# One-hots of a gate table stored contiguously per token, with PSUM written in steps of four

## The chip, the cores and the metric

One Trainium2 chip, one core of it. The metric is the device time of one launch in microseconds, lower is better. Engines are named as the profile names them: PE (TensorE; PEld its weight loads), DVE (VectorE), ACT (ScalarE), POOL (GpSimd), SP (SyncE, which only issues DMAs here).

## What is computed

A decoder trunk of two layers over 512 tokens of width 1024: a mixer of four kinds of attention, then a PEER expert layer with 16384 experts. The change lies in the expert layer alone:

```
v1, i1 = top_k(s1, 16);  v2, i2 = top_k(s2, 16)          # per token and head, 128 keys each
top_s, top_j = top_k(v1[..., :, None] + v2[..., None, :], 16)
eid  = take_along_axis(i1 * 128 + i2, top_j)             # 8 heads x 16 = 128 experts per token
gate = softmax(top_s)
act  = gelu(einsum('cd,ced->ce', h, u[eid]))
out  = einsum('ce,ced->cd', gate * act, v[eid])
```

The kernel does this in a dense way for the first 384 tokens (three blocks of 128): it multiplies all tokens with all experts and weights the result with a *gate table*. For a token t the table is a 128 x 128 matrix: entry (a, b) is the gate of expert a * 128 + b, or zero. It is the product of two one-hot matrices, one of them scaled by the gates.

## The kernel before

The expert layer, per layer of the trunk, has a *stage* in which the gate table is built while the first experts' products with u already run, and a long stage after it that multiplies by the table and by v.

Each token block is turned by PE so that the 128 picks of a token lie on the partitions (`turn`). `turned_out` (L1614) stores the two numbers of each pick as `iT` (float16) and its gate as a float16 pair `gT` (high and low part, with `gF` and `gL` in float32). Then, for each batch b of eight tokens, 48 batches per layer:

- `g_ones` (L1628, DVE) compares the numbers with a row of 0 to 127 (`iota4`) and writes both one-hots of eight tokens, tile `o`: 2048 elements per partition.
- `g_scale` (L1635) multiplies the one-hot of the first number by the high (q = 0) and by the low (q = 1) part of the gate, tile `og`. It is one DVE instruction of 1024 elements, or, on ACT, eight of 128 with the token's gate as the scale.
- `g_mm` (L1648, PE, twice per batch): for each of four tokens two matmuls of 128 x 128 (high and low part added up), into a quarter of one PSUM bank `psa`.
- `g_out` (L1656, ACT) evicts that bank of four tokens into `gs`, in which the 32 tokens of a group are innermost. Every eighth eviction completes a group, and `g_put` (SP) sends it to `gdram`.

Meanwhile PE computes `u_mm` of one expert after another (24 matmuls of 384 columns, `psb`), for which ACT writes `uh` (L1347) and DVE `ul` (L1350), and ACT applies the gelu (`act`, L1363). Only 27 experts run beside the table; four more are held back until the last table matmul. DVE also decodes the picks of the later token blocks (`oh`, `pr`, `cid`, `ts`).

The order of all this on each engine is fixed when the program is built: the class `Plan` simulates it with costs written in the source, and `plan.run()` emits the instructions in the order found. The costs of the table's steps are these:

```
one = plan.add(due, lambda b=b: g_ones(b), ("W", 1.135), after=(ids_,), take=("o",))
hi = plan.add(due + 1, lambda e, b=b: g_scale(b, 0, E[e]), [("W", 0.602), ("S", 2.4)], after=(one, gts), take=("og",))
lo = plan.add(due + 1, lambda e, b=b: g_scale(b, 1, E[e]), [("W", 0.602), ("G", 2.3), ("S", 2.4)][:LA], after=(hi,))
```

Tile `o` has three buffers and `og` two, so work on batch b + 2 can enter `og` only when the matmuls of batch b are done.

After the stage, `gq_load` (L1799) reads the table back from `gdram`, `w_mul` (L1804) multiplies it with `act`, and the products with v follow.

Of the kernel before, what the change touches and what calls it, by code (L numbers as in the profile page):

```python
# [12 lines left out]
F16 = mybir.dt.float16  # L13
# [3 lines left out]
AF = mybir.ActivationFunctionType  # L17
ALU = mybir.AluOpType
# [22 lines left out]
GL = (3, 2, 3, 2, 2)  # L41
OA = (1, 0)
GSC = 2.0 ** 14
# [52 lines left out]
def bc(ap, shape):  # L96
    return ap.to_broadcast(shape)
# [1229 lines left out]
def peer(nc, tc, I, l, xd, fh, fl, h3, closing, q0, w012, both, wq_mm, right, hp, up, small, bank, mm3, iota128, pos, ident, dram, grow, ada, more, rows_out):  # L1327
    V, S, G, PE, SY = nc.vector, nc.scalar, nc.gpsimd, nc.tensor, nc.sync
# [35 lines left out]
    with tc.tile_pool(name=f"Q{l}", bufs=1) as qp:  # L1364
# [4 lines left out]
        wp = wcm.__enter__()  # L1369
# [105 lines left out]
        for h in range(8):  # L1475
            t0 = 10.2 * (h - 1)
            if h > 2:
                loads[h] = plan.add(t0 - 16, lambda h=h: wq_load(h), ("Q", 3.2), take=("wr",))
                wsplit[h] = []
                for half in range(2):  # L1480
                    a = plan.add(t0 - 7 + half, lambda h=h, half=half: wq_part(h, half, S), ("S", 1.0), after=(loads[h], wtake[h] if half else None), take=("w",) if half == 0 else ())
# [19 lines left out]
            for i in range(NT):  # L1501
# [6 lines left out]
                b = plan.add(at + 0.5, lambda h=h, i=i: key_best(h, i), ("V", 2.03), after=(m, lasts[-1] if lasts else None),  # L1508
                             take=("top",) if i == 0 else (), give=(("b" if h < KB else "a", src),) if h < KB or i % 2 else ())
# [7 lines left out]

        def turn_over():

            nonlocal wp, dp, iT, gT, gL, gF, iota4, pos8  # L1520
            wcm.__exit__(None, None, None)
            for cm in closing:
                cm.__exit__(None, None, None)
            rcm, rp = right(tc.tile_pool(name=f"ring{l}", bufs=1))
            ring.append(rp)
            cms.extend([rcm, tc.tile_pool(name=f"Q2{l}", bufs=1), tc.tile_pool(name=f"G{l}", bufs=1), tc.manual_schedule()])
            wp, dp = cms[1].__enter__(), cms[2].__enter__()
            cms[3].__enter__()
            iT = wp.tile([128, 96, 2, 4], F16, name="iT")
            gT = wp.tile([128, 2, 384], F16, name="gT")  # L1530
            gL, gF = (wp.tile([128, 384], F32, name=q) for q in ("gL", "gF"))
            iota4 = wp.tile([128, 128, 4], F16, name="iota4")
            G.tensor_copy(iota4, bc(iota128[:, :, None], [128, 128, 4]))
            pos8 = wp.tile([128, sum(NSEL), 8], F16, name="pos8")
            G.tensor_copy(pos8, bc(pos[:, :, None], [128, sum(NSEL), 8]))

        dp = iT = gT = gL = gF = iota4 = pos8 = None
        ready = plan.add(B0, turn_over, ("none", 0), after=list(kmm.values()) + dense)
        if True:
            picked, cids, ohs, prs, turned = {}, {}, {}, {}, {}  # L1540
# [73 lines left out]
            def turned_out(i, part):  # L1614
                cs, ps = slice(i * 128, (i + 1) * 128), turned[i]
                if part == 0:
                    V.tensor_copy(iT[:, 32 * i:32 * i + 32].rearrange("p g a t -> p a g t"), ps[:, 0:256].rearrange("p (a g t) -> p a g t", a=2, t=4))
                elif part == 1:
                    S.activation(gF[:, cs], ps[:, 256:384], AF.Copy, scale=GSC)
                    S.activation(gT[:, 0, cs], gF[:, cs], AF.Copy)  # L1620
                else:
                    V.tensor_sub(gL[:, cs], gF[:, cs], gT[:, 0, cs])
                    V.tensor_copy(gT[:, 1, cs], gL[:, cs])

            gst, gps, oo, gg = {}, {}, {}, {}
            NG = NTG * TG // 4

            def g_ones(b):  # L1628

                o = oo[b] = dp.tile([128, 4, 128, 4], F16, name="o", tag="o", bufs=GL[0])  # L1630
                shp = [128, 4, 128, 4]
                V.tensor_tensor(out=o, in0=bc(iota4[:, None], shp), op=ALU.is_equal,
                                in1=bc(iT[:, 2 * b:2 * b + 2].rearrange("p g a t -> p (g a) t")[:, :, None, :], shp))

            def g_scale(b, q, eng):  # L1635

                if q == 0:
                    gg[b] = dp.tile([128, 2, 2, 128, 4], F16, name="og", tag="og", bufs=GL[1])
                h, o = gg[b], oo[b].rearrange("p (g a) c t -> p g a c t", a=2)[:, :, 0]
                g = gT[:, q, 8 * b:8 * b + 8].rearrange("p (g t) -> p g t", t=4)  # L1640
                if eng is S:
                    for t in range(8):
                        g, t4 = divmod(t, 4)
                        S.activation(h[:, q, g, :, t4], oo[b][:, 2 * g, :, t4], AF.Copy, scale=(gL if q else gF)[:, 8 * b + t:8 * b + t + 1])  # L1644
                else:
                    eng.tensor_mul(h[:, q], o, bc(g[:, :, None, :], [128, 2, 128, 4]))

            def g_mm(j):  # L1648
                b, g = divmod(j, 2)
                o, h = oo[b], gg[b]  # L1650
                gps[j] = bank("a")
                for t in range(4):
                    for q in range(2):
                        PE.matmul(gps[j][:, t * 128:(t + 1) * 128], lhsT=o[:, 2 * g + 1, :, t], rhs=h[:, q, g, :, t], start=q == 0, stop=q == 1)  # L1654

            def g_out(j):  # L1656
                tg, t4 = divmod(j, TG // 4)
                if t4 == 0:
                    gst[tg] = dp.tile([128, 128, TG], F32, name="gs", tag="gs", bufs=GL[4])
                S.activation(gst[tg][:, :, 4 * t4:4 * t4 + 4].rearrange("p a t -> p t a"), gps.pop(j).rearrange("p (t a) -> p t a", t=4), AF.Copy, scale=1 / GSC)  # L1660

            def g_put(tg):
                SY.dma_start(gdram[tg], gst.pop(tg))
# [2 lines left out]
            turns, a, f = [], None, None  # L1666
            for i in range(NT):
                due, d = B0 + QD[i], QD[4]
# [3 lines left out]
                for q in range(4):  # L1672
                    a = plan.add(due + d * q, lambda e, i=i, q=q: ids(i, q, E[e]), [("G", 0.2 * len(SELB[q]) + NSEL[q] / 60), ("W", 0.08 * len(SELB[q]) + NSEL[q] / 240)],
                                 after=(head, a), take=("cid",))
                    b = plan.add(due + d * (1 + q), lambda i=i, q=q: places(i, q), dv(16 * NSEL[q], True), after=(t,), take=("oh",))
                    c = plan.add(due + d * (2 + q), lambda i=i, q=q: chosen(i, q), dv(16 * NSEL[q], True), after=(a, b), take=("pr",), give=(("cid", a), ("oh", b)))
                    red.append(plan.add(due + d * (3 + q), lambda i=i, q=q: decoded(i, q), ("W", 0.2 + 22 * NSEL[q] / 960), after=(c,), give=(("pr", c),)))
                f = plan.add(due + d * 7, lambda i=i: finish(i), ("V", 1.5), after=red + [ex, f], give=(("p", head),) if i == 3 else ())
                if i < 3:
                    f = plan.add(due + d * 8, lambda i=i: turn(i), ("PE", 0.65), after=(f,), take=("a",), give=(("p", head),))  # L1680
                    n = plan.add(due + d * 8, lambda i=i: turned_out(i, 0), dv(256), after=(f,))
                    b = plan.add(due + d * 8, lambda i=i: turned_out(i, 1), ("S", 0.5), after=(f,))
                    c = plan.add(due + d * 8, lambda i=i: turned_out(i, 2), ("V", 0.45), after=(b, n), give=(("a", f),))
# [106 lines left out]
    with tc.tile_pool(name=f"D{l}", bufs=1) as dp, ExitStack() as order:  # L1790
# [136 lines left out]
        with tc.tile_pool(name=f"X{l}", bufs=1) as xp:  # L1927
# [28 lines left out]
            if state is None:  # L1956
                scale, rest = evac(3)
                for i in range(2):
# [4 lines left out]
                    scale, rest = nxt  # L1963
# [152 lines left out]
```

## Time and profile before

| | |
|---|---|
| median of 3 runs | 3342.16 us (3340.18 to 3348.39) |
| the profiled execution | 3341.59 us, span of the core 3339.8 us |
| busy share of the span | PE 95%, PEld 84%, DVE 77%, ACT 45%, POOL 26% |
| mean granted TensorE clock | 0.971 of full speed |
| instructions | 48260 |

The span runs from the first to the last instruction. The table's stage is some 200 us of it per layer: about 520 to 720 us in the first layer and about 2170 to 2368 us in the second. A share over the whole span says little about it, so stretches of it are read by themselves below. Where the timeline gives one row for several instructions (x4), its length goes from the first start to the last end; instructions of one engine overlap a little, so the pace of a run is the distance from start to start, and not the length of one.

### The profile page before, as it was taken

The numbers are of one execution on the slowest core, as the hardware profiler recorded it, in microseconds if no ns is written. First come the engines' busy times: TensorE is split into PE (matmuls) and PEld (weight loads), VectorE is DVE, ScalarE is ACT, GpSimd is POOL, SyncE is SP. The second block draws the span as 40 slices with busy tenths as digits, with TensorE's granted clock in tenths as the row PEclk, the third lists the DMA queues.
The fourth block names the chain that finished last, engine by engine and source line by source line (L and its number), as shares of the span: only waits on it lengthen the run. The fifth ranks groups of instructions, "written<-read, shape, count | busy, mean of one in ns | idle before, by whom it ended". The sixth has DMA issues, their size and how long they took to land.

```text
span 3339.8 us, 48260 instructions
## 1 busy us (share of the span) xinstructions
PE 3183.5 (95%) x17540; PEld 2816.0 (84%) x17540; DVE 2585.4 (77%) x5528; ACT 1516.9 (45%) x2763; POOL 851.9 (26%) x682
## 2 busy tenths in 40 slices
PE   6999999979999999999999999998899999999998
PEld 6876879869989999998888668897799899999987
DVE  7767798858878888786666868988578787878856
ACT  3267527873333333333432864289533333333333
POOL 1300210004433343341022002100234344444400
PEclk9999999869999999999999999997899999999999
DMA  8402304459889989896654032144688899999954
GB/s 281 145 9 95 128 33 152 177 217 334 324 323 336 347 322 335 323 352 232 201 177 142 1 133 103 51 163 184 255 316 328 311 336 321 326 325 325 323 183 163
DMA packets 291343, 762.77 MB, mean 228 GB/s; under 512 B 23832, under 2 KB 130968, under 8 KB 285984
## 3 DMA queue, kind: packets, MB, share of 16 engines
q1 hardware_dynamic: 217376, 491.22, 42.3%
q0 software_dynamic: 73728, 268.47, 21.8%
q8 instruction: 137, 2.24, 0.3%
q14 instruction: 102, 0.84, 0.1%
HBM read 700.86 MB, written 58.74 MB: 227 GB/s over the span
## 4 chain that ended last, share of the span: by engine, by line
PE 75%; DVE 11%; ACT 8%; DMA 4%; issue 2%; POOL 0%; SPq 0%; DVEq 0%; ACTq 0%; POOLq 0%
PE psa L204 12%; PE psa L205 12%; PE psa L203 12%; PE psb L203 10%; PE psb L205 9%; PE psb L204 9%; ACT gs L1660 3%; PE psa L1654 2%; ACT og L1644 2%; PE psa L863 2%; PE psa L896 1%; DMA gq<-gdram 1%; DVE s L1437 1%; DMA wr<-in_w_in 1%; ACT P L877 1%
## 5 line engine op out<-in xcount | busy, mean ns | idle before, releaser
L203 PE MATMUL psb<-bh,uh 128*128 128x384 f32 x2048 | 692.0, 338 | 3.0 <-ACT act L1363 1.2
L205 PE MATMUL psb<-bh,ul 128*128 128x384 f32 x2048 | 688.9, 336 | 3.0 <-DVE ul L1350 3.0
L204 PE MATMUL psb<-bl,uh 128*128 128x384 f32 x2048 | 687.4, 336 | 0.0
L203 PE MATMUL psa<-vh,wdh 128*128 128x512 f32 x1512 | 590.8, 391 | 16.5 <-ACT wdh L1815 16.5
L205 PE MATMUL psa<-vh,wdl 128*128 128x512 f32 x1512 | 594.1, 393 | 0.0
L204 PE MATMUL psa<-vl,wdh 128*128 128x512 f32 x1512 | 593.8, 393 | 0.0
L1750 POOL DMA_INDIRECT gt<-in_peer_u,eid x256 | 341.6, 1334 | 726.3 <-DVE gt L1770 233.7
L1815 ACT ACTIVATE wdh<-act 128x384 fp32r<-128x384 f32 x252 | 132.1, 524 | 862.2 <-PE psa L204 640.6
L1750 POOL DMA_INDIRECT gt<-in_peer_v,eid x256 | 322.7, 1261 | 425.3 <-DVE a L1775 195.7
L203 PEld LDWEIGHTS psb<-bh,uh 128*128 128x128 f32 x2048 | 386.6, 189 | 13.2 <-DVE arow L250 2.6
L204 PEld LDWEIGHTS psb<-bl,uh 128*128 128x128 f32 x2048 | 386.1, 189 | 7.3
L205 PEld LDWEIGHTS psb<-bh,ul 128*128 128x128 f32 x2048 | 385.5, 188 | 4.7 <-DVE ul L1350 4.3
L1350 DVE TENSOR_TENSOR ul<-ur,uh 128x1024 fp32r<-128x1024 f32 x246 | 301.6, 1226 | 100.1 <-ACT uh L1347 87.8
L1816 DVE TENSOR_TENSOR wdl<-act,wdh 128x384 fp32r<-128x384 f32 x252 | 140.9, 559 | 286.6 <-ACT wdh L1815 272.1
L203 PEld LDWEIGHTS psa<-vh,wdh 128*128 128x128 f32 x1512 | 285.3, 189 | 72.2 <-ACT wdh L1815 17.1
L205 PEld LDWEIGHTS psa<-vh,wdl 128*128 128x128 f32 x1512 | 285.0, 188 | 60.1
L1827 DVE TENSOR_TENSOR vl<-vr,vh 128x1024 fp32r<-128x1024 f32 x252 | 307.8, 1221 | 33.0 <-ACT vh L1824 22.7
L204 PEld LDWEIGHTS psa<-vl,wdh 128*128 128x128 f32 x1512 | 285.1, 189 | 56.1
L1775 DVE SCALAR_TENSOR_TENSOR a<-gt,w,a 128x1024 f32<-128x1024 f32 x254 | 325.6, 1282 | 0.8
L1770 DVE SCALAR_TENSOR_TENSOR gt<-gt,h 128x1024 f32<-128x1024 f32 x256 | 310.9, 1220 | 0.0
L1347 ACT ACTIVATE uh<-ur 128x1024 fp32r<-128x1024 f32 x256 | 268.4, 1049 | 76.0 <-PE psb L204 64.2
L1363 ACT ACTIVATE act<-psb 128x384 f32<-128x384 f32 x256 | 126.8, 495 | 340.3 <-PE psb L205 340.2
(387 smaller groups left out, 5374.2 us busy)
## 6 DMA issues: line engine op xcount, KB each, us to landing
ur<-in_peer_uT SPq DMA_DIRECT2D x256, 512.0 KB
vr<-in_peer_v SPq DMA_DIRECT2D x256, 512.0 KB
gdram<-gs SPq DMA_DIRECT2D x24, 2048.0 KB
gq<-gdram SPq DMA_DIRECT2D x64, 768.0 KB
O<-in_ada_w SPq DMA_DIRECT2D x48, 512.0 KB
gt<-in_ada_w SPq DMA_DIRECT2D x32, 512.0 KB
wr<-in_w_q SPq DMA_DIRECT2D x14, 1024.0 KB
wr<-in_w_out SPq DMA_DIRECT2D x16, 512.0 KB
```

What stands on the lines that cost most here:

```text
L203: PE.matmul(ps, lhsT=wh, rhs=mh, start=first, stop=False)
L204: PE.matmul(ps, lhsT=wh, rhs=ml, start=False, stop=False)
L205: PE.matmul(ps, lhsT=wl, rhs=mh, start=False, stop=last)
L1347: S.activation(uspl[e][0], uraw[e], AF.Copy)
L1350: eng.tensor_sub(uspl[e][1], uraw.pop(e), uspl[e][0])
L1363: S.activation(acts[e], ups.pop(e)[:, :384], AF.Gelu_apprx_tanh)
L1750: G.indirect_dma_start(out=t, out_offset=None, in_=I["peer_u" if kind == "u" else "peer_v"], in_offset=bass.IndirectOffsetOnAxis(ap=eid3[: ...
L1770: V.scalar_tensor_tensor(t, t, 1.0, h3, op0=ALU.mult, op1=ALU.mult, accum_out=d3[:, s:s + 1])
L1775: V.scalar_tensor_tensor(a3, t, w3[:, s:s + 1], a3, op0=ALU.mult, op1=ALU.add)
L1815: S.activation(wh, w, AF.Copy)
L1816: V.tensor_sub(wl, w, wh)
L1827: V.tensor_sub(vspl[e][1], vraw.pop(e), vspl[e][0])
```

## The change

The one-hots of a token become contiguous (token, then which of the two numbers, then 128 columns), where before four tokens were interleaved element by element. For that the numbers and gates are stored twice side by side (`iT` and `gT` end in a dimension of 2), the row of 0 to 127 once (`iota16`, seen as 64 pairs), and DVE's operands are described in innermost runs of 2 elements, where they were runs of 4. PE then reads both its operands with step 1 (before: step 4) and writes each token's 128 columns into PSUM with a step of four columns (before: contiguous). ACT's eviction reads the bank in order and writes runs of four neighbouring words into `gs` (before: single words, 128 bytes apart).

```
-            iT = wp.tile([128, 96, 2, 4], F16, name="iT")
-            gT = wp.tile([128, 2, 384], F16, name="gT")
+            iT = wp.tile([128, 384, 2, 2], F16, name="iT")
+            gT = wp.tile([128, 2, 384, 2], F16, name="gT")
...
-            G.tensor_copy(iota4, bc(iota128[:, :, None], [128, 128, 4]))
+            G.tensor_copy(iota16, iota128.rearrange("p (c d) -> p c d", d=2))
...
-                    V.tensor_copy(iT[:, 32 * i:32 * i + 32].rearrange("p g a t -> p a g t"), ps[:, 0:256].rearrange("p (a g t) -> p a g t", a=2, t=4))
+                    V.tensor_copy(iT[:, cs].rearrange("p t a d -> p a t d"), bc(ps[:, 0:256].rearrange("p (a t) -> p a t", a=2)[:, :, :, None], [128, 2, 128, 2]))
...
-                    S.activation(gT[:, 0, cs], gF[:, cs], AF.Copy)
+                    S.activation(gT[:, 0, cs], bc(gF[:, cs, None], [128, 128, 2]), AF.Copy)
...
-                o = oo[b] = dp.tile([128, 4, 128, 4], F16, name="o", tag="o", bufs=GL[0])
-                shp = [128, 4, 128, 4]
-                V.tensor_tensor(out=o, in0=bc(iota4[:, None], shp), op=ALU.is_equal,
-                                in1=bc(iT[:, 2 * b:2 * b + 2].rearrange("p g a t -> p (g a) t")[:, :, None, :], shp))
+                o = oo[b] = dp.tile([128, 8, 2, 128], F16, name="o", tag="o", bufs=GL[0])
+                shp = [128, 16, 64, 2]
+                V.tensor_tensor(out=o.rearrange("p t a (c d) -> p (t a) c d", d=2), in0=bc(iota16[:, None], shp), op=ALU.is_equal,
+                                in1=bc(iT[:, 8 * b:8 * b + 8].rearrange("p t a d -> p (t a) d")[:, :, None, :], shp))
...
-                        S.activation(h[:, q, g, :, t4], oo[b][:, 2 * g, :, t4], AF.Copy, scale=(gL if q else gF)[:, 8 * b + t:8 * b + t + 1])
+                        S.activation(h[:, q, t], o[:, t], AF.Copy, scale=(gL if q else gF)[:, 8 * b + t:8 * b + t + 1])
                 else:
-                    eng.tensor_mul(h[:, q], o, bc(g[:, :, None, :], [128, 2, 128, 4]))
+                    pair = lambda x: x.rearrange("p t (c d) -> p t c d", d=2)
+                    eng.tensor_mul(pair(h[:, q]), pair(o), bc(gT[:, q, 8 * b:8 * b + 8, None], [128, 8, 64, 2]))
...
-                        PE.matmul(gps[j][:, t * 128:(t + 1) * 128], lhsT=o[:, 2 * g + 1, :, t], rhs=h[:, q, g, :, t], start=q == 0, stop=q == 1)
+                        PE.matmul(gps[j].rearrange("p (a t) -> p a t", t=4)[:, :, t], lhsT=o[:, 4 * g + t, 1], rhs=h[:, q, 4 * g + t], start=q == 0, stop=q == 1)
...
-                S.activation(gst[tg][:, :, 4 * t4:4 * t4 + 4].rearrange("p a t -> p t a"), gps.pop(j).rearrange("p (t a) -> p t a", t=4), AF.Copy, scale=1 / GSC)
+                S.activation(gst[tg][:, :, 4 * t4:4 * t4 + 4], gps.pop(j).rearrange("p (a t) -> p a t", t=4), AF.Copy, scale=1 / GSC)
```

The planner's costs are not touched, and no instruction moves: each engine issues the same number of instructions in the same order, with other access patterns. A piece of ACT's order in the first layer shows it, where the third token block is turned (`gF` and `gT` are its gates).

```order
 L1363 ACTIVATE act<-psb 128x384
-L1644 ACTIVATE og<-o,gL 128x128 x8
-L1660 ACTIVATE gs<-psa 128x4x128 x3
+L1642 ACTIVATE og<-o,gL 128x128 x8
+L1659 ACTIVATE gs<-psa 128x128x4 x3
 L1619 ACTIVATE gF<-psa 128x128
```

Eight scalings and three evictions stand in the same places; the eviction's pattern turns from four tokens of 128 columns to 128 columns of four tokens, and the source lines shift by one or two.

## Rows read from the trace of the kernel before

**Rows 1.** The page: busy time, share and instructions of each engine.

```profile
PE 3183.5 (95%) x17540; PEld 2816.0 (84%) x17540; DVE 2585.4 (77%) x5528; ACT 1516.9 (45%) x2763; POOL 851.9 (26%) x682
```

**Rows 2.** Windows, all engines: start and end, length, busy time (instructions), clock.

```profile
541.00:641.00 100.00, 98.92 (x656) 95.78 (x654) 81.34 (x141) 86.12 (x149) 5.74 (x2) 0.97 0.49 180
641.00:722.00 81.00, 61.95 (x436) 52.60 (x434) 61.84 (x96) 79.98 (x152) 0.00 (x0) 0.62 0.42 175
...
2290.00:2368.00 78.00, 58.96 (x420) 49.62 (x419) 60.84 (x94) 77.97 (x150) 0.00 (x0) 0.63 0.41 169
```

**Rows 3.** The same windows for the evictions into `gs` alone: ACT's busy time.

```profile
641.00:722.00 81.00, 49.97 (x51) 0.62 0.42 175
```

**Rows 4.** Timeline of ACT: start, length, instruction, count.

```profile
658.49 2.66 ACT L1644 ACTIVATE og<-o,gL 128x128 f16<-128x128 f16 x8
660.89 3.90 ACT L1660 ACTIVATE gs<-psa 128x512 f32<-128x512 f32 x4
664.60 2.66 ACT L1644 ACTIVATE og<-o,gL 128x128 f16<-128x128 f16 x8
```

**Rows 5.** Timeline of PE beside experts.

```profile
613.71 0.34 PE L205 MATMUL psb<-bh,ul 128*128 128x384 f32 x1
613.88 2.06 PE L1654 MATMUL psa<-og,o 128*128 128x128 f16 x16
```

**Rows 6.** Timeline of PE without experts, with its idle time ahead and what ended it.

```profile
659.07 4.42 PE L1654 MATMUL psa<-og,o 128*128 128x128 f16 x32 [1.90 <-ACT og L1644]
```

**Rows 7.** Timeline of DVE in the same loop.

```profile
661.51 0.69 DVE L1646 TENSOR_TENSOR og<-o,gT 128x1024 f16<-128x1024 f16 x1 [1.43 <-PE psa L1654]
662.12 2.51 DVE L1632 TENSOR_TENSOR o<-iota,iT 128x2048 f16<-128x2048 f16 x2
664.54 0.68 DVE L1646 TENSOR_TENSOR og<-o,gT 128x1024 f16<-128x1024 f16 x1
...
665.67 0.69 DVE L1646 TENSOR_TENSOR og<-o,gT 128x1024 f16<-128x1024 f16 x1
```

**Rows 8.** Chain that ended last, behind the table's last matmul: start, length.

```profile
720.00 6.99 DMA gdram<-gs
...
728.40 16.84 DMA gq<-gdram
...
745.27 0.57 DVE act L1806
```

**Rows 9.** Timelines of ACT in the mixer: contiguous writes.

```profile
200.02 1.05 ACT L802 ACTIVATE PT<-psa 128x512 f32<-128x512 f32 x2
200.97 0.38 ACT L877 ACTIVATE P<-P,nm 128x128 f32<-128x128 f32 x1
...
235.90 1.27 ACT L886 ACTIVATE P<-P,rz 128x128 f32<-128x128 f32 x4
```

**Rows 10.** Instructions on tile `o` (ns: shortest/median/longest), and `ul` by form.

```profile
L1654 PE MATMUL psa<-og,o x1536: 273/297/303, 525.6 to 2362.9; 128*128 128x128 f16 x192
L1644 ACT ACTIVATE og<-o,gL x352: 531/565/635, 532.1 to 2360.4; 128x128 f16<-128x128 f16 x176
L1646 DVE TENSOR_TENSOR og<-o,gT x146: 678/687/697, 525.0 to 2359.5; 128x1024 f16<-128x1024 f16 x146
L1632 DVE TENSOR_TENSOR o<-iota,iT x96: 1211/1219/3444, 521.1 to 2353.8; 128x2048 f16<-128x2048 f16 x96
...
L1350 DVE TENSOR_TENSOR ul<-ur,uh 128x1024 fp32r<-128x1024 f32 x246 | 301.6, 1226 | 100.1 <-ACT uh L1347 87.8 <-issue 12.2
```

**Rows 11.** PE's matmuls by form: count, busy us, mean ns of one.

```profile
L203 PE MATMUL psb<-bh,uh 128*128 128x384 f32 x2048 | 692.0, 338 | 3.0 <-ACT act L1363 1.2 <-ACT uh L1347 1.1 <-DVE arow L250 0.8
L203 PE MATMUL psa<-vh,wdh 128*128 128x512 f32 x1512 | 590.8, 391 | 16.5 <-ACT wdh L1815 16.5
```

**Rows 12.** Chain that ended last, early in the stage.

```profile
551.20 3.71 ACT gs L1660 x4
...
555.29 0.69 PE psb L203
```

More of the change, by code (lines that the diff above doesn't have):

```diff
@@ L1518, in turn_over @@
         def turn_over():
-            nonlocal wp, dp, iT, gT, gL, gF, iota4, pos8
+            nonlocal wp, dp, iT, gT, gL, gF, iota16, pos8
             wcm.__exit__(None, None, None)
@@ L1528, in turn_over @@
             cms[3].__enter__()
-            iT = wp.tile([128, 96, 2, 4], F16, name="iT")
-            gT = wp.tile([128, 2, 384], F16, name="gT")
+            iT = wp.tile([128, 384, 2, 2], F16, name="iT")
+            gT = wp.tile([128, 2, 384, 2], F16, name="gT")
             gL, gF = (wp.tile([128, 384], F32, name=q) for q in ("gL", "gF"))
-            iota4 = wp.tile([128, 128, 4], F16, name="iota4")
-            G.tensor_copy(iota4, bc(iota128[:, :, None], [128, 128, 4]))
+            iota16 = wp.tile([128, 64, 2], F16, name="iota16")
+            G.tensor_copy(iota16, iota128.rearrange("p (c d) -> p c d", d=2))
             pos8 = wp.tile([128, sum(NSEL), 8], F16, name="pos8")
             G.tensor_copy(pos8, bc(pos[:, :, None], [128, sum(NSEL), 8]))
-        dp = iT = gT = gL = gF = iota4 = pos8 = None
+        dp = iT = gT = gL = gF = iota16 = pos8 = None
         ready = plan.add(B0, turn_over, ("none", 0), after=list(kmm.values()) + dense)
@@ L1616, in turned_out @@
                 if part == 0:
-                    V.tensor_copy(iT[:, 32 * i:32 * i + 32].rearrange("p g a t -> p a g t"), ps[:, 0:256].rearrange("p (a g t) -> p a g t", a=2, t=4))
+                    V.tensor_copy(iT[:, cs].rearrange("p t a d -> p a t d"), bc(ps[:, 0:256].rearrange("p (a t) -> p a t", a=2)[:, :, :, None], [128, 2, 128, 2]))
                 elif part == 1:
                     S.activation(gF[:, cs], ps[:, 256:384], AF.Copy, scale=GSC)
-                    S.activation(gT[:, 0, cs], gF[:, cs], AF.Copy)
+                    S.activation(gT[:, 0, cs], bc(gF[:, cs, None], [128, 128, 2]), AF.Copy)
                 else:
-                    V.tensor_sub(gL[:, cs], gF[:, cs], gT[:, 0, cs])
-                    V.tensor_copy(gT[:, 1, cs], gL[:, cs])
+                    V.tensor_sub(gL[:, cs], gF[:, cs], gT[:, 0, cs, 0])
+                    V.tensor_copy(gT[:, 1, cs], bc(gL[:, cs, None], [128, 128, 2]))
             gst, gps, oo, gg = {}, {}, {}, {}
@@ L1628, in g_ones @@
             def g_ones(b):
-                o = oo[b] = dp.tile([128, 4, 128, 4], F16, name="o", tag="o", bufs=GL[0])
-                shp = [128, 4, 128, 4]
-                V.tensor_tensor(out=o, in0=bc(iota4[:, None], shp), op=ALU.is_equal,
-                                in1=bc(iT[:, 2 * b:2 * b + 2].rearrange("p g a t -> p (g a) t")[:, :, None, :], shp))
+                o = oo[b] = dp.tile([128, 8, 2, 128], F16, name="o", tag="o", bufs=GL[0])
+                shp = [128, 16, 64, 2]
+                V.tensor_tensor(out=o.rearrange("p t a (c d) -> p (t a) c d", d=2), in0=bc(iota16[:, None], shp), op=ALU.is_equal,
+                                in1=bc(iT[:, 8 * b:8 * b + 8].rearrange("p t a d -> p (t a) d")[:, :, None, :], shp))
             def g_scale(b, q, eng):
                 if q == 0:
-                    gg[b] = dp.tile([128, 2, 2, 128, 4], F16, name="og", tag="og", bufs=GL[1])
-                h, o = gg[b], oo[b].rearrange("p (g a) c t -> p g a c t", a=2)[:, :, 0]
-                g = gT[:, q, 8 * b:8 * b + 8].rearrange("p (g t) -> p g t", t=4)
+                    gg[b] = dp.tile([128, 2, 8, 128], F16, name="og", tag="og", bufs=GL[1])
+                h, o = gg[b], oo[b][:, :, 0]
                 if eng is S:
                     for t in range(8):
-                        g, t4 = divmod(t, 4)
-                        S.activation(h[:, q, g, :, t4], oo[b][:, 2 * g, :, t4], AF.Copy, scale=(gL if q else gF)[:, 8 * b + t:8 * b + t + 1])
-                else:
-                    eng.tensor_mul(h[:, q], o, bc(g[:, :, None, :], [128, 2, 128, 4]))
+                        S.activation(h[:, q, t], o[:, t], AF.Copy, scale=(gL if q else gF)[:, 8 * b + t:8 * b + t + 1])
+                else:
+                    pair = lambda x: x.rearrange("p t (c d) -> p t c d", d=2)
+                    eng.tensor_mul(pair(h[:, q]), pair(o), bc(gT[:, q, 8 * b:8 * b + 8, None], [128, 8, 64, 2]))
             def g_mm(j):
```

## The prediction, made before the changed kernel ran

> **What bounds the kernel now.** I read the page first: PE is busy for 95% of the span [rows 1], which would say that only PE's work counts. But the change lies in one stage of some 200 us per layer, so I cut that stage into stretches. Up to 641 us PE is busy for 98.92 of 100 us, beside ACT's 86.12 and DVE's 81.34: PE interleaves experts with table matmuls, and PE ends last. [...] So each layer has a stretch A bound by PE and a stretch B bound by ACT.
>
> In stretch B, ACT's timeline repeats every 6.11 us (658.49 to 664.60): eight scalings at a pace of 2.40/8 = 0.30 us, then four evictions at 3.71/4 = 0.93 us [rows 4]. One loop serves two batches. PE waits 1.90 us in it for ACT's scalings [rows 6], DVE waits 1.43 us for PE [rows 7]. Behind the stage the chain of waits goes from ACT's last eviction through the DMA of the last group (720.00, 6.99 us) and the load of the table (16.84 us) to DVE's first multiplication at 745.27 [rows 8]. Nothing there waits for the held experts, so what ACT's last eviction gains, the rest of the layer gains too.
>
> **The change part by part**, for one layer.
>
> *The eviction.* It keeps its 512 elements and its place, but writes runs of four words. Nearest row with contiguous writes from PSUM: two evictions of 128x512 start at 200.02 and ACT's next instruction at 200.97, so a pace of 0.48 [rows 9]. Bounds are 0.48 and today's 0.93; I take 0.48, since a run of four neighbours is nearer to a contiguous row than to single words 128 bytes apart.
>
> *The scalings on ACT.* Today one takes 565 ns [rows 10] but the next starts 0.30 us later. In the mixer four contiguous ones of 128x128 with the same kind of scale take 1.27 us together, and one such instruction 0.38 [rows 9]: a pace of (1.27 - 0.38)/3 = 0.30. So contiguity does not lift the pace; it can shorten the delay of the first result, by up to 565 - 380 = 0.18 us. Bounds 0.28 and 0.30: no gain in ACT's work.
>
> *What the loop becomes.* ACT's own work falls from 6.11 to 2.40 + 4 x 0.48 = 4.32 us. DVE's is about 4.85 us (661.51 to 665.67, plus 0.69, with a short wait for a buffer in it) [rows 7]. But the order is fixed, and a chain through ACT and PE closes the loop: first scaling to first matmul 0.58 us (658.49 to 659.07, [rows 4, 6]), seven more scalings 2.10, then the other batch's 16 matmuls at PE's pace of 0.117, which is 1.87, the length of the last one 0.30 [rows 10], and its eviction 0.48: together 5.33 us, or 5.15 with the shorter first result. I take 5.25. That saves 0.86 per loop. The stretch has 51 evictions [rows 3]: ten such loops, then a tail that ends in seven evictions in a row. Loops: -8.6 us. In the tail the evictions shrink by 7 x 0.45 = 3.2, and the one between the last two sets of scalings by another 0.45: -3.6. Together -12.2. Counter-check: 51 evictions x 0.45 are 23 us of ACT's work, of which the chain hands back 10 x (5.25 - 4.32) = 9.3, which leaves -13.7. I take -12.5.
>
> *Early in the stage* four evictions (3.71 us) hold ACT, and PE's next expert starts at 555.29 right behind them [rows 12]. Four at 0.48 would release PE up to 1.8 us earlier; I count -1.7.
>
> *The matmuls.* Their number stays: 768 per layer, half of 1536 [rows 10], of which 51 x 8 = 408 belong to stretch B and 360 to stretch A. Sixteen take (2.06 - 0.30)/15 = 0.117 us each [rows 5]. What the new patterns do, no row shows, so I bound it. From below: an expert's matmul of 384 columns starts 0.17 us before its successor (613.71 to 613.88), 0.45 ns per column, so 128 columns could pass in 0.058 us. That today's pace is not near this has a sign in the lengths: 384 columns take 338 ns and 512 take 391 [rows 11], 0.41 ns per column; carried down to 128 that is 232 ns, and the table's matmuls take 297 [rows 10]. Something costs them 65 ns, and the stepped operands may be it. From above: ACT's stepped writes cost 0.93/0.48 = 1.9 times the contiguous ones; as a factor on today's matmul that is 0.226 us. PE loses two stepped inputs and gets one stepped output. I take a pace of 0.113, near today's row, because one stepped operand remains: 360 x 0.004 = -1.4 us in stretch A; in stretch B it is within the 5.25.
>
> [...] No run here shows a matmul with a stepped output so far.
>
> *DVE.* `g_ones` takes 1219 ns for 2048 elements and a scaling 687 ns for 1024, while `ul`, with 4-byte elements, takes 1226 ns for 1024 [rows 10]: the 16-bit operations run at twice the elements per time, in runs of 4. With runs of 2 I take the same lengths; the other bound is the pace of `ul`, 1.2 ns per element, 2.3 and 1.23 us. [...]
>
> *Storing in pairs* writes 256 more elements in the copy of the numbers and 128 more in those of the gates, three times per layer. By `ul`'s row 256 elements are 0.3 us; only the first block's copy lies ahead of the first one-hot. +0.3. POOL's smaller copy of the 0-to-127 row gives nothing: POOL is busy for 5.74 of 100 us in stretch A and on none of the chains above [rows 2].
>
> Sum per layer: -12.5 - 1.7 - 1.4 + 0.3 = -15.3 us; two layers -30.6. The profiled execution took 3341.59 us (span 3339.8), 0.6 below the median of 3342.16, so the forecast is 3311 us. A measurement of this kernel can tell about 0.3%, 10 us, from no change.
>
> **The rivals.**
>
> *PE gets quick.* If the 65 ns are due to the stepped inputs and a stepped output costs nothing, the pace goes towards 0.058. Stretch A could lose 360 x 0.059 = 21 us, but DVE is busy for 81.34 of 100 there with a fixed order, so I grant 13. In stretch B the chain falls below DVE's work and the loop ends near 4.85: ten loops -12.6, tail -4.6. With the early -1.7 and the +0.3 that is -31.6 per layer, 3278 us, and 3262 if all 21 come through. For it: the lengths of rows 11. Against it: one stepped operand remains.
>
> *PE gets slow* (the other side). Each written column costs more than today's, up to 0.226 us per matmul. PE ends last in stretch A, so every nanosecond counts there: 360 x 0.109 = +39 us. In stretch B PE's two matmuls per token (0.45) then outlast a scaling (0.30), and the loop grows to about 0.6 + 8 x 0.45 + 16 x 0.226 + 0.8 = 8.6 us, +25 over ten loops. Per layer some +65, 3470 us at that bound. It decides from where the costs eat the -13.9 of the other terms: about 360 + 10 x 18 + 20 = 560 matmuls lie on the path, so at 0.117 + 0.025 = 0.142 us. [...]
>
> *DVE loses its double pace on runs of two.* 48 one-hots at +1.07 and 73 scalings at +0.54 are 91 us of DVE work per layer in two stretches where DVE is idle for 18.7 + 19.2 = 38 us [rows 2]; if all of that were filled, +53 per layer, 3448 us. Against it: the pace is the same to a few ns for `og` and `o` in runs of 4, and nothing in the rows hints at a limit on the run.
>
> *The eviction doesn't get shorter*, since its runs of four still lie 128 bytes apart: the loop stays at 6.11 and only small terms are left, 3340 us.
>
> **How the numbers follow.** The forecast (matmul pace 0.100 to 0.130, eviction near 0.5) gets 0.50; its own range is 3298 to 3323. PE quick 0.26, PE slow 0.13, DVE at single pace 0.05, eviction unchanged 0.06. Predicted is the likeliest, 3311. Faster by over 0.3%: 0.50 + 0.26 + 0.02 of PE slow (paces between 0.130 and 0.135) = 0.78. Within 0.3%: the unchanged eviction and the paces around the break-even, 0.07. Slower: 0.15. The range takes in all of the forecast and nearly all of PE quick, down to 3262, and reaches up to 3345 for the unchanged eviction; outside are most of PE slow, DVE's loss and a rest, 0.19.
>
> **What the new profile would show.** Eviction right: a pace near 0.48 where it was 0.93. Loop right: ACT's sets of scalings some 5.2 us apart, and ACT waiting for PE before its last evictions. Matmuls: 16 in about 1.8 us beside an expert; 0.9 to 1.3 would be PE quick, over 2.3 PE slow. DVE right: `o` near 1.22 and `og` near 0.69 us. Wrong would be the whole reading if the stage shrinks and the first multiplication after the table's load does not come earlier by as much.

## The result, and the profile after

| | before | changed |
|---|---|---|
| median of 4 runs each | 3341.47 us | 3296.93 us (3293.22 to 3299.51) |
| ratio | | 0.9862, 95% interval 0.9845 to 0.9879 |
| profiled execution | 3341.59 us, span 3339.8 | 3297.31 us, span 3295.5 |
| mean granted TensorE clock | 0.971 | 0.991 |

The change takes off 44.3 us of the profiled execution, where 30.6 were forecast. First the page's busy line, which answers to [rows 1]: ACT has lost 83 us of busy time, PE 28, DVE 2.

```profile
PE 3155.2 (96%) x17540; PEld 2798.2 (85%) x17540; DVE 2583.2 (78%) x5528; ACT 1433.5 (43%) x2763; POOL 846.2 (26%) x682
```

The windows of the stage, for [rows 2] (start and end, length, then the busy time of PE, PEld, DVE, ACT and POOL, then clock, DMA share and GB/s). The stretch without experts now ends at 703 us.

```profile
541.00:641.00 100.00, 99.34 (x696) 96.78 (x694) 86.01 (x153) 72.54 (x153) 5.58 (x2) 1.00 0.51 186
641.00:703.00 62.00, 49.13 (x406) 42.82 (x405) 59.89 (x92) 56.56 (x150) 0.00 (x0) 1.00 0.53 219
2264.00:2324.00 60.00, 47.14 (x389) 40.83 (x387) 58.28 (x90) 54.98 (x147) 0.00 (x0) 1.00 0.53 220
```

Beside the experts PE still ends last (99.34 of 100 us). Without them it is no longer ACT: DVE is busy for 59.89 of 62 us, ACT for 56.56, and the granted clock is 1.00, where it was 0.62. The evictions alone, for [rows 3], are down from 49.97 to 27.59 us:

```profile
641.00:703.00 62.00, 27.59 (x51) 1.00 0.53 219
```

The instructions on the tiles `o` and `gs` (ns: shortest/median/longest), for [rows 10]:

```profile
L1653 PE MATMUL psa<-og,o x1536: 269/314/315, 531.5 to 2323.8; 128*128 128x128 f16 x192
L1642 ACT ACTIVATE og<-o,gL x352: 384/391/433, 537.2 to 2319.0; 128x128 f16<-128x128 f16 x176
L1645 DVE TENSOR_TENSOR og<-o,gT x146: 674/685/694, 531.3 to 2321.6; 128x1024 f16<-128x1024 f16 x146
L1632 DVE TENSOR_TENSOR o<-iota,iT x96: 1210/1219/3426, 527.3 to 2316.9; 128x2048 f16<-128x2048 f16 x96
...
L1659 ACT ACTIVATE gs<-psa x192: 573/597/623, 533.6 to 2324.1; 128x512 f32<-128x512 f32 x192
```

DVE's two operations took no harm from runs of two (1219 and 685 ns, before 1219 and 687). A matmul got longer (314 ns, before 297), yet the next one starts sooner: sixteen beside the experts, for [rows 5], take 1.92 us where they took 2.06, so the pace is (1.92 - 0.314)/15 = 0.107 us, before 0.117. The timeline of PE:

```profile
614.47 1.92 PE L1653 MATMUL psa<-og,o 128*128 128x128 f16 x16
```

The loop without experts, for [rows 4, 6, 7] (timeline of ACT, DVE and PE: start, length, instruction, count, and the idle time ahead with what ended it):

```profile
656.22 2.05 ACT L1659 ACTIVATE gs<-psa 128x512 f32<-128x512 f32 x4
...
658.13 2.47 ACT L1642 ACTIVATE og<-o,gL 128x128 f16<-128x128 f16 x8
658.85 3.54 PE L1653 MATMUL psa<-og,o 128*128 128x128 f16 x31 [0.87 <-DVE og L1645]
...
660.47 1.69 ACT L1659 ACTIVATE gs<-psa 128x512 f32<-128x512 f32 x3
660.68 1.23 DVE L1632 TENSOR_TENSOR o<-iota,iT 128x2048 f16<-128x2048 f16 x1 [0.15 <-PE psa L1653]
661.82 0.69 DVE L1645 TENSOR_TENSOR og<-o,gT 128x1024 f16<-128x1024 f16 x1
662.43 0.58 DVE L1579 TENSOR_REDUCE ts<-pr 128x32 f32<-128x256 int16 x1
662.43 0.60 ACT L1659 ACTIVATE gs<-psa 128x512 f32<-128x512 f32 x1 [0.28 <-PE psa L1653]
...
662.92 1.28 DVE L1645 TENSOR_TENSOR og<-o,gT 128x1024 f16<-128x1024 f16 x2
...
663.66 3.54 PE L1653 MATMUL psa<-og,o 128*128 128x128 f16 x31 [0.81 <-DVE og L1645]
```

Follow the circle: PE starts at 658.85; 1.83 us later it has freed a tile `o`, and DVE's `g_ones`, which waited for that, starts (660.68); then come a scaling (661.82), an operation of the decoding (662.43), the other scaling (662.92), and PE starts again at 663.66: 1.83 + 1.14 + 0.61 + 0.49 + 0.74 = 4.81 us. Over eight loops, PE's starts lie (693.81 - 653.97)/8 = 4.98 us apart, before 6.11. Each of the nine starts of PE waits for DVE; ACT waits 0.28 us for PE, ahead of the last of its four evictions. Four evictions in a row take 2.05 us, a pace of (2.05 - 0.60)/3 = 0.48 us, before 0.93.

Behind the stage, for [rows 8], the chain that ended last (start, length, what):

```profile
698.84 0.60 DVE og L1645
699.44 0.90 DVE pr L1571
700.34 0.61 DVE og L1645
701.00 1.81 PE psa L1653 x15
702.83 0.61 ACT gs L1659
703.46 6.25 DMA gdram<-gs
...
711.13 18.64 DMA gq<-gdram
729.79 0.57 DVE act L1805
```

A single eviction ends the stage where seven in a row did, and DVE and PE stand ahead of it. From the DMA of the last group to the first multiplication there are 26.3 us, before 25.3, so the stage's gain arrives there but for 1 us.

### The profile page after: what moved, and what is told of

It reads as the page before. It is cut to its first block, busy times and chain, and to the rows that moved or that the text cites. A ratio compares the mean times of both kernels' runs of the same rounds, so it can differ in the third digit from the quotient of the medians.

```text
span 3295.5 us, 48260 instructions
## 1 busy us (share of the span) xinstructions
PE 3155.2 (96%) x17540; PEld 2798.2 (85%) x17540; DVE 2583.2 (78%) x5528; ACT 1433.5 (43%) x2763; POOL 846.2 (26%) x682
## 4 chain that ended last, share of the span: by engine, by line
PE 77%; DVE 13%; DMA 4%; ACT 3%; issue 2%; POOL 0%; SPq 0%; DVEq 0%; POOLq 0%; ACTq 0%
PE psa L204 12%; PE psa L205 12%; PE psa L203 12%; PE psb L203 10%; PE psb L205 10%; PE psb L204 10%; PE psa L1653 4%; PE psa L863 2%; PE psa L896 1%; DVE o L1632 1%; DMA gq<-gdram 1%; DMA wr<-in_w_in 1%; DMA O<-in_ada_w 1%; DVE s L1437 1%; DVE og L1645 1%
## 5 line engine op out<-in xcount | busy, mean ns | idle before, releaser
L1769 DVE SCALAR_TENSOR_TENSOR gt<-gt,h 128x1024 f32<-128x1024 f32 x256 | 310.8, 1219 | 0.0
```

What stands on the lines that cost most here:

```text
L1769: V.scalar_tensor_tensor(t, t, 1.0, h3, op0=ALU.mult, op1=ALU.mult, accum_out=d3[:, s:s + 1])
```

## Where the 44.3 us came from

I cut both executions at the first table matmul, at the end of the experts, and where ACT's last eviction hands over to the DMA:

| us | before | changed | difference | forecast |
|---|---|---|---|---|
| layer 1, beside experts | 525.6 to 640.39: 114.8 | 531.5 to 640.27: 108.8 | -6.0 | -2.8 |
| layer 1, without | to 720.00: 79.6 | to 703.46: 63.2 | -16.4 | -12.5 |
| layer 2, beside experts | 2175.6 to 2287.89: 112.3 | 2152.9 to 2261.57: 108.7 | -3.6 | -2.8 |
| layer 2, without | to 2367.62: 79.7 | to 2324.7: 63.1 | -16.6 | -12.5 |
| all the rest | 2953.4 | 2951.7 | -1.7 | 0 |

The rest is +5.9 us ahead of the first stage and -7.6 behind it, with no table work in it. In the thirteen profiled executions of this study the first table matmul starts anywhere from 523.2 to 533.6 us, so this is how far one execution differs from another. The two stages explain 42.6 us. What needs an explanation is why the stretch without experts gave 4 us per layer more than forecast, and which side of the matmul sets its pace.

## Experiments

In the first expectations, **S** is the theory that the stepped output in PSUM sets the matmuls' pace of 0.107 us, and **W** its rival, by which something else sets it and the pace stays when the output is made contiguous. A second question, whether the loop is closed by DVE and PE or by ACT and PE, comes last. The experiments are told by subject; E3 is the third kernel that ran. All paces below are worked out as above, from sixteen matmuls beside an expert, between 598 and 622 us. The granted clock there is 1.00 in both kernels of the change (598 to 622 us), in E3 (541 to 641 us) and in E7 (536 to 636 us). In the others whose pace is given, the experts' matmuls next to the sixteen start 0.17 us apart, as they do in the kernel before (613.71 to 613.88), so I put no difference in pace down to the clock. The ratios of the experiments are to the kernel before, of which seven executions go with each set of runs (medians 3341.36 to 3342.61 us).

### The output in PSUM, and who undoes the interleaving

E1: the changed kernel, with PSUM written contiguously as before, and with the eviction of before.

```
-  PE.matmul(gps[j].rearrange("p (a t) -> p a t", t=4)[:, :, t], lhsT=...
+  PE.matmul(gps[j][:, t * 128:(t + 1) * 128], lhsT=...
-  S.activation(gst[tg][:, :, 4*t4:4*t4+4], gps.pop(j).rearrange("p (a t) -> p a t", t=4), ...
+  S.activation(gst[tg][:, :, 4*t4:4*t4+4].rearrange("p a t -> p t a"), gps.pop(j).rearrange("p (t a) -> p t a", t=4), ...
```

> The changed kernel, but PSUM is written contiguously and the eviction writes single words 128 bytes apart, both as in the kernel before; the operands of the matmuls stay contiguous. Theory S (the stepped output sets the matmuls' pace of 0.107 us in the changed kernel): with all three operands contiguous the pace falls to between 0.058 and 0.08 us. Theory W (the pace has another cause, such as the weight loads; the step of the output is free): the pace stays at 0.107. In both the eviction is back at 0.93 us and the loop without experts at about 6.05 us, bound by ACT. Time by S about 3310 us, by W about 3328 us.

Measured: 3307.43 us, ratio 0.990 [0.9883, 0.9918]. The rows on `o` and `gs` of this kernel:

```profile
L1653 PE MATMUL psa<-og,o x1536: 216/219/314, 527.0 to 2328.0; 128*128 128x128 f16 x192
...
L1659 ACT ACTIVATE gs<-psa x192: 1015/1150/1367, 528.6 to 2331.4; 128x512 f32<-128x512 f32 x192
```

Sixteen matmuls take 1.07 us, a pace of (1.07 - 0.219)/15 = 0.057, and one takes 219 ns where it took 314. So the stepped output made 0.107, and W falls (E2, which keeps the fast eviction, has the same pace). The eviction is back at 1150 ns, and without experts ACT binds again: its sets of scalings start at 645.17 and 650.93, 5.76 us apart, somewhat less than the 6.05 expected, since four evictions in a row now take 3.73 us, a pace of 0.86.

E2: PSUM contiguous too, but ACT reads it with a step of 128 columns and keeps writing runs of four words.

```
-  S.activation(gst[tg][:, :, 4*t4:4*t4+4], gps.pop(j).rearrange("p (a t) -> p a t", t=4), ...
+  S.activation(gst[tg][:, :, 4*t4:4*t4+4], gps.pop(j).rearrange("p (t a) -> p a t", t=4), ...
```

> The changed kernel, but PSUM is written contiguously and ACT does the reordering: it reads the bank with a step of 128 columns and writes the same runs of four words. Theory S: matmul pace 0.058 to 0.08 us; the stretch beside the experts loses 6 to 18 us per layer, time 3260 to 3285 us if ACT's stepped read keeps the pace of 0.48 us. Theory W: matmul pace 0.107, time 3297 us within 5. If ACT pays for the step when it reads (pace 0.9), the loop without experts goes back towards 6.1 us and the time is over 3310 us in either theory.

Measured: 3263.9 us, ratio 0.9772 [0.9755, 0.9788], faster than both kernels of the change. The rows on `o` and `gs`, and the windows with and without experts:

```profile
L1653 PE MATMUL psa<-og,o x1536: 216/219/314, 528.4 to 2289.9; 128*128 128x128 f16 x192
...
L1659 ACT ACTIVATE gs<-psa x192: 570/592/638, 530.1 to 2290.2; 128x512 f32<-128x512 f32 x192
```

```profile
541.00:624.00 83.00, 78.58 (x648) 75.91 (x646) 79.63 (x134) 65.72 (x148) 5.25 (x2) 0.98 0.59 216
625.00:686.00 61.00, 39.80 (x411) 34.49 (x411) 59.81 (x96) 56.67 (x150) 0.00 (x0) 0.76 0.54 225
```

The eviction that reads with steps takes 592 ns, the one that reads in order 597: on ACT the stepped read is free, on PE the stepped write costs 50 ns per matmul. DVE is now the busiest engine in both windows: 79.63 of 83 us, just above PE's 78.58, and 59.81 of 61.

E4: the changed kernel with PSUM written in steps of two columns instead of four (two tokens interleaved).

```
-  PE.matmul(gps[j].rearrange("p (a t) -> p a t", t=4)[:, :, t], lhsT=...
+  PE.matmul(gps[j].rearrange("p (h a d) -> p h a d", h=2, d=2)[:, t // 2, :, t % 2], lhsT=...
...
```

The eviction reads the pairs back into order and writes runs of four words, as before; its edit is left out here.

> The changed kernel with PSUM written in steps of two columns (two tokens side by side, in each half of a bank), the eviction reading pairs and writing the same runs of four words. Theory S, if the pace depends on whether neighbouring columns are written one after the other: 0.107 us still, time 3297 us within 5. If it depends on how far apart the columns lie, between 0.058 and 0.107 and the time below 3290 us. Theory W: 0.107 us.

Measured: 3294.57 us, ratio 0.9864 [0.9847, 0.9881], 314 ns per matmul, sixteen in 1.92 us: the pace of step four, 0.107.

E9: PSUM in pairs, two neighbouring columns of a token side by side, then those of the next token.

```
-  PE.matmul(gps[j].rearrange("p (a t) -> p a t", t=4)[:, :, t], lhsT=...
+  PE.matmul(gps[j].rearrange("p (a t d) -> p a t d", t=4, d=2)[:, :, t], lhsT=...
...
```

Here too the eviction undoes it as it reads, and its edit is left out.

> The changed kernel with PSUM written in pairs: two neighbouring columns of a token stand side by side (8 bytes), then the pairs of the other three tokens follow; ACT's eviction undoes it while it reads and still writes runs of four words. It asks what makes a stepped output slow. If it is that two columns written one after the other never share 8 bytes (steps of two and of four columns both gave a pace of 0.107 us): the pace falls to 0.057 and the time to that of the kernel with contiguous PSUM, 3264 us. If any output that isn't one run is slow: 0.107 and 3297 us, like the changed kernel. [...]

Measured: 3267.43 us, ratio 0.9775 [0.9757, 0.9793]. The timeline of PE beside the experts:

```profile
602.55 1.07 PE L1653 MATMUL psa<-og,o 128*128 128x128 f16 x16
```

Full pace, 0.057, though the output is still spread over the whole bank. So it isn't the spread that costs: the slow patterns are the two in which no column has its neighbour beside it, and pairs are enough. Of the two cases in the expectation, the first came about. Pairs that begin at an odd column were not tried.

### The eviction alone

E3: the kernel before, with nothing but its `g_mm` and `g_out` changed; the operands stay interleaved by four.

```
-  PE.matmul(gps[j][:, t * 128:(t + 1) * 128], lhsT=o[:, 2 * g + 1, :, t], rhs=h[:, q, g, :, t], ...
+  PE.matmul(gps[j].rearrange("p (a t) -> p a t", t=4)[:, :, t], lhsT=o[:, 2 * g + 1, :, t], rhs=h[:, q, g, :, t], ...
```

> The kernel before with only the output side of the change: PSUM written in steps of four columns, eviction in runs of four words; one-hots and gates interleaved by four tokens as before. The working of the prediction gives a loop of 5.33 us at a matmul pace of 0.117 (ACT's first result still takes 565 ns), so -12 us per layer without experts and nothing beside them: about 3317 us. If stepped inputs and a stepped output add up instead of hiding each other, the pace is 0.14 or more, the stretch beside the experts gets longer, and the time is 3325 us or more.

Measured: 3306.17 us, ratio 0.9895 [0.9879, 0.9912]. So this output side of the change takes off 35 us by itself. E1 is its other side, contiguous operands with the output and the eviction of before, and takes off 34 by itself (3341.36 to 3307.43). Together they take off 44.5 and not 69, because the stepped output takes back from PE much of what the contiguous operands give it: beside the experts layer 1 takes 114.8 us in the kernel before, 100.3 in E1 (527.0 to 627.31) and 108.8 in the changed kernel. E2, with a contiguous output and a fast eviction, takes off 77. The timeline of PE in E3, beside experts and at the beginnings of two loops:

```profile
604.26 2.05 PE L1654 MATMUL psa<-og,o 128*128 128x128 f16 x16
...
655.73 4.16 PE L1654 MATMUL psa<-og,o 128*128 128x128 f16 x32 [0.85 <-DVE og L1646]
660.67 4.15 PE L1654 MATMUL psa<-og,o 128*128 128x128 f16 x32 [0.79 <-DVE og L1646]
```

With stepped inputs and a stepped output the pace is (2.05 - 0.299)/15 = 0.117, as with stepped inputs alone: the costs do not add up, the larger one hides the other. And PE waits for DVE here too. Seven loops, from 655.73 to 691.65, take 5.13 us each; the seven with the same work on DVE in the changed kernel, from 658.85 to 693.81, take 4.99. The circle through 16 matmuls asks for 16 x 0.010 = 0.16 us, and the difference is 0.14.

### Which input was slow

E5 and E6 take the kernel of E2 and let PE read one operand with a step of four elements, as in the kernel before: E5 the weights, E6 the moving operand.

```
-  lhsT=o[:, 4 * g + t, 1]
+  lhsT=o.rearrange("p (g x) a (c s) -> p g (x a c) s", x=2, s=4)[:, t, :, 2 * g + 1]      # E5
-  rhs=h[:, q, 4 * g + t]
+  rhs=h[:, q, 4 * g:4 * g + 4].rearrange("p x (c s) -> p (x c) s", s=4)[:, :, t]          # E6
```

> The kernel with contiguous PSUM and the stepped read by ACT (3263.9 us, matmul pace 0.057 us), in which the table matmuls alone read their weights with a step of four elements; they thereby read other elements of the same tile of one-hots, so the values of the gate table are changed and the time alone is looked at. It asks which of the two stepped inputs made the pace of 0.117 us in the kernel before. If the weights made it: a pace near 0.117, PEld instructions near the 117 ns of the kernel before instead of 98, and a time near 3300 us, since the third kernel (only the eviction changed, pace 0.117) took 3306. If the moving operand made it: a pace of 0.057 to 0.060 and 3264 us. If each adds half: near 0.087 and some 3275 us.

> The same kernel with contiguous weights, in which the table matmuls alone read their moving operand with a step of four elements; it reads other elements of the same scaled tile, so the values of the gate table are changed and the time alone is looked at. If the moving operand made the pace of 0.117 us: a pace near 0.117, weight loads still near 98 ns, and some 3300 us. If the weights made it: 0.057 to 0.060 and 3264 us. If each adds half: near 0.087 and some 3275 us. If the sum over both kernels is well over 0.117 + 0.057, either of the two steps is enough by itself and they hide each other.

Measured: 3262.82 us with stepped weights, 3305.25 with the stepped moving operand, one run each. The rows on `o`, first of E5, then of E6:

```profile
L1653 PEld LDWEIGHTS <-o x1536: 110/113/152, 524.8 to 2288.4; 128*128 128x128 f16 x192
L1653 PE MATMUL psa<-og,o x1536: 216/219/314, 524.8 to 2288.5; 128*128 128x128 f16 x192
```

```profile
L1653 PEld LDWEIGHTS <-o x1536: 95/116/136, 526.6 to 2330.2; 128*128 128x128 f16 x192
L1653 PE MATMUL psa<-og,o x1536: 272/294/299, 526.6 to 2330.3; 128*128 128x128 f16 x192
```

Stepped weights lengthen their load from 98 to 113 ns and leave the pace at (1.09 - 0.219)/15 = 0.058. The moving operand gives 2.02 us for sixteen: (2.02 - 0.294)/15 = 0.115. So the moving operand alone makes the pace of before (0.117), all but 0.002 us.

E10 and E11 change the moving operand's pattern again: a step of two elements (4 bytes), and pairs of neighbours 16 bytes apart, which cover as much memory as the step of four.

```
+  rhs=h[:, q, 4*g + 2*(t // 2):4*g + 2*(t // 2) + 2].rearrange("p x (c s) -> p (x c) s", s=2)[:, :, t % 2]   # E10
+  rhs=h[:, q, 4*g:4*g + 4].rearrange("p x (c s d) -> p (x c) s d", s=4, d=2)[:, :, t]                        # E11
```

> The kernel with contiguous PSUM and the stepped read by ACT, in which the table matmuls read their moving operand with a step of two float16 elements (4 bytes) instead of four; it reads other elements of the same scaled tile, so the values of the gate table are changed and the time alone is looked at. With a step of four the pace was 0.115 us. If neighbours have to lie side by side, as for the output: about 0.115 and 3305 us. If it counts how many of the elements read lie close together: somewhere between 0.057 and 0.115, and 3264 to 3290 us.

> The same, but the moving operand is read in pairs of neighbours, with a step of eight float16 elements (16 bytes) from pair to pair; again other elements of the same tile, so the time alone is looked at. It reads the same stretch of memory per column as the step of four does. If neighbours that lie side by side are enough, as asked of the output: 0.057 us and 3264 us. If the length of the stretch that is read decides: 0.115 us and 3305 us.

Measured, one run each: 3274.5 us with step two, whose sixteen matmuls take 1.10 us, a pace of (1.10 - 0.219)/15 = 0.059; 3300.37 us with pairs, 2.02 us and 0.115. E10's time lies 11 us above E2's, but single executions of E8, whose matmuls take 219 ns as E2's do, and of E9, which has E2's pace, took as long (3275.7 and 3273.4 us), so the pace is what tells. The input asks something other than the output: neighbours side by side don't help. In these four patterns the pace goes with the stretch of memory that the 128 elements take up: 256 and 512 bytes pass at full pace (0.057 and 0.059 us), 1024 bytes at half of it (0.115), whether in steps or in pairs. Stretches between 512 and 1024 bytes were not tried.

### Who closes the loop

E7: the changed kernel with four buffers for `o`; planner and order stay. E8: the same edit in the kernel of E2.

```
-  o = oo[b] = dp.tile([128, 8, 2, 128], F16, name="o", tag="o", bufs=GL[0])
+  o = oo[b] = dp.tile([128, 8, 2, 128], F16, name="o", tag="o", bufs=GL[0] + 1)
```

> The changed kernel with one buffer more for the tile of one-hots (four instead of three); order and planner unchanged. In the changed kernel the loop without experts takes 4.98 us. If it is closed by the circle PE's last matmuls, DVE's next one-hot that waits for the freed buffer, scaling, PE: the fourth buffer opens that circle, the loop falls to DVE's own work of 4.5 to 4.85 us, which is 10 x 0.13 to 0.5 us per layer, so 3288 to 3294 us. If it is closed by a chain through ACT and PE, as the prediction had it, or by DVE's work alone: no change, 3297 +- 3 us.

> The fastest kernel so far (contiguous PSUM, stepped read by ACT, 3263.9 us) with a fourth buffer for the tile of one-hots. There DVE is busy for 59.81 of 61 us in the stretch without experts. If DVE's own work alone sets that stretch: no change, 3264 +- 3 us. If waits for a buffer of one-hots still stand between DVE's instructions, above all beside the experts: some us less, 3255 to 3261 us.

Measured: 3290.49 us for E7, ratio 0.985 [0.983, 0.987]. That interval overlaps with the changed kernel's, so the time alone does not decide; the trace does. DVE and PE in the loop:

```profile
654.38 2.35 DVE L1632 TENSOR_TENSOR o<-iota,iT 128x2048 f16<-128x2048 f16 x2
656.65 0.68 DVE L1645 TENSOR_TENSOR og<-o,gT 128x1024 f16<-128x1024 f16 x1
657.25 0.57 DVE L1579 TENSOR_REDUCE ts<-pr 128x32 f32<-128x256 int16 x1
657.74 1.28 DVE L1645 TENSOR_TENSOR og<-o,gT 128x1024 f16<-128x1024 f16 x2
...
658.47 3.75 PE L1653 MATMUL psa<-og,o 128*128 128x128 f16 x32 [0.82 <-DVE og L1645]
```

DVE's wait for PE ahead of the second `o` is gone, and PE's starts lie (687.19 - 649.27)/8 = 4.74 us apart, 0.24 less than with three buffers. The stage of layer 1 goes from 172.0 us (531.5 to 703.46) to 169.6 (527.0 to 696.59): 2.4 us, which is 10 x 0.24. The circle through the buffer of `o` did close the loop, and was worth 0.24 us of it. What is left, 4.74 us, is DVE's own work.

E8, 3267.26 us, ratio 0.9776 [0.9758, 0.9793], can't be told from E2 by the time, but it can by the trace. A set of two `o` on DVE in the loop, first of E2, then the same of E8:

```profile
643.35 2.55 DVE L1632 TENSOR_TENSOR o<-iota,iT 128x2048 f16<-128x2048 f16 x2
...
648.35 2.35 DVE L1632 TENSOR_TENSOR o<-iota,iT 128x2048 f16<-128x2048 f16 x2
```

In E2 four of eight sets take 2.55 us, so there too the second `o` waits 0.20 us for a buffer; in E8 all take 2.35. Eight loops take 4.84 us each in E2 (638.52 to 677.23) and 4.74 in E8 (643.71 to 681.63), the figure of E7. That is 1 us per layer, too little for the times to show.

## Why the prediction was right, and which of its steps failed

The measured 3296.93 us lies 1 us below the forecast's own range, 3298 to 3323, although both of its conditions came about (a pace of 0.100 to 0.130, an eviction near 0.5). It lies in the stated range because that reached down to 3262 for *PE quick*, which did not come about. So the direction and the main cause were foreseen; that the 14 us beyond the forecast stayed inside the range is luck.

*What bounds the kernel* and *where the gain arrives* were right: PE ended the stretch beside the experts (the prediction's A, read in layer 1) and ACT's evictions the one without them (its B, read in both layers) [rows 2], and what that second stretch gained came through to the first multiplication in both layers.

*The eviction* was right to the digit: 0.48 us. So were *DVE in runs of two* (no cost) and *storing in pairs*: the copy of the numbers went from 420 to 683 ns, 0.26 us against 0.3.

*What the loop becomes* failed in its mechanism. I closed the loop by a chain through ACT and PE that held the other batch's 16 matmuls: 5.33 us, shaded to 5.25. But the order on ACT is another one. These are four evictions between two sets of scalings in the changed kernel's order, numbers kept:

```
528 L1642 ACTIVATE og_7244<-o_7217,gL_5064 128x128 x8
529 L1659 ACTIVATE gs_7280<-psa_7247 128x128x4
530 L1659 ACTIVATE gs_7280<-psa_7258 128x128x4
531 L1659 ACTIVATE gs_7280<-psa_7282 128x128x4
532 L1659 ACTIVATE gs_7280<-psa_7294 128x128x4
533 L1642 ACTIVATE og_7305<-o_7276,gL_5064 128x128 x8
```

`psa_7282` and `psa_7294` are the banks of `og_7244`, the batch that ACT itself has just scaled. The next scalings wait for that batch's evictions, and the other batch's matmuls run ahead of it, under ACT's scalings: in the rows above PE starts at 658.85, while ACT scales from 658.13 to 660.60. Without them my chain is 0.58 + 2.10 + 0.30 + 0.48 = 3.46 us, less than ACT's own 4.32, and it closes nothing. What does is DVE: its own work, 4.74 us by E7, for which I had 4.85 with a short wait in it, and 0.24 us for the buffer of `o`, which I named in passing and did not price. The loop came to 4.98; ten loops give -11.3 instead of -8.6, and the tail, where one eviction is left behind the last matmul, the other -5 of the 16.4, instead of -3.6.

*The matmuls*: the mechanism was right (two stepped inputs go, one stepped output comes, and the gain is small), the size was not. A pace of 0.107 instead of 0.113 makes 360 x 0.010 = -3.6 us instead of -1.4. It is what layer 2's stretch beside the experts lost, with no sign of the -1.7 of the next term. The stepped output does cost (0.107 against 0.057 us), but that did not decide the sign, since the moving operand's step had cost more (0.115 to 0.117) and the two don't add up (0.117 in E3).

*Early in the stage* I counted -1.7 us from four evictions, and that term came to nothing. In [rows 12] the expert at 555.29 follows behind them, but PE was idle there for only 0.57 us, and that was all there was to gain. It went, and PE waits about as much longer for DVE elsewhere (0.82 and 0.66 us ahead of two batches, before 0.48 and 0.51). Layer 1 lost 2.4 us more than layer 2, for a reason that no term held. These are the first expert's matmul behind that wait in the kernel before and the window around it, in layer 1 and then in layer 2:

```profile
555.29 0.69 PE L203 MATMUL psb<-bh,uh 128*128 128x384 f32 x1 [0.57 <-ACT act L1363]
541.00:561.00 20.00, 18.91 (x118) 18.18 (x116) 15.85 (x21) 19.10 (x38) 0.00 (x0) 0.83 0.57 224
...
2205.38 0.45 PE L203 MATMUL psb<-bh,uh 128*128 128x384 f32 x1 [0.59 <-ACT act L1363]
2191.00:2211.00 20.00, 18.90 (x135) 17.98 (x134) 15.75 (x20) 19.18 (x39) 0.00 (x0) 1.00 0.55 216
```

The waits are alike, but the granted clock is 0.83 in layer 1 and 1.00 in layer 2. From the start behind the wait to the eighteenth after it PE takes 5.82 us in layer 1 (555.29 to 561.11) and 3.24 in layer 2 (2205.38 to 2208.62). Those 2.6 us account for the 2.4; in the changed kernel the clock is 1.00 in both layers, and their stretches beside the experts are equally long. Why it fell in one layer and not in the other stays open. That this gain hides 2.4 of the 3.4 us that the term promised over both layers is luck too.

*The rivals.* PE quick did not come about, and for the reason given against it: one stepped operand remained. E2, which takes it away, gives 3263.9 us, in the 3262 to 3278 worked out for that rival. PE slow would have needed 0.142 us. DVE at single pace and an unchanged eviction are out by the rows above.

The 13.7 us between forecast and profiled execution are thus: 8.0 from the stretches without experts, 4.0 from those beside them, 1.7 from the rest.

## What to carry to other kernels

When data must be re-ordered between PE and ACT, let the engine do it that pays nothing for it: here ACT's read of PSUM, which took 592 ns in steps of 128 columns and 597 in order, while PE lost half its pace where it wrote single columns two or four apart (0.107 us against 0.057). If PE must interleave, pairs of columns were enough here (0.057). And when a bound falls, work out the next one from the order on each engine, bank by bank: here it was DVE's own work and a buffer circle, both seen beforehand, and a chain that the order ruled out was put in their place.

## What the hardware showed that I had not expected

- A matmul of 128 x 128 in float16 started every 0.057 us with contiguous operands, beside the experts (E1, E2). A moving operand with a step of 8 bytes made that 0.115 (E6), of 4 bytes 0.059 (E10); pairs 16 bytes apart 0.115 (E11). Stepped weights made 0.058 (E5). An output with a step of two or four columns made 0.107 (E4, the changed kernel), in pairs 0.057 (E9). A stepped moving operand and a stepped output together, with stepped weights, made 0.117 (E3), not their sum.
- The granted clock in the stretch without experts was 0.62 before (PE busy for 61.95 of 81 us), 1.00 in the changed kernel (49.13 of 62) and 0.76 in E2 (39.80 of 61), where its matmuls are shortest. There the lower clock costs, by my estimate from the loops of E2 and E8 (4.84 and 4.74 us), at most the 0.10 us per loop that DVE waits for PE; the rest of the loop is DVE's own work.
